# Side work of a finished chunk handed out as a pipeline of stages

## The chip, the core and the metric

The kernel runs on one NeuronCore of a Trainium2 chip. The metric is device time in microseconds (us) of the whole program. Engines: TensorE (PE, matrix products; PEld are its weight loads), VectorE (DVE), ScalarE (ACT), GpSimdE (POOL), and SyncE (SP), which here issues every DMA.

## The reference

One encoder layer and a final normalisation, for two groups of tokens (512 and 1024 of them, width 1024) with shared weights. What matters here, for the hidden state `h` of one group:

```python
h = h + jnp.concatenate([o_attn, o_pool], axis=-1) @ w_out
m = _rmsnorm(h, norm_mlp_g)
h = h + jnp.square(jax.nn.relu(m @ w_up)) @ w_down
gate = jax.nn.sigmoid((_rmsnorm(h, norm_ple_g) @ w_ple_gate).astype(jnp.float32)).astype(h.dtype)
h = h + gate * (p_i @ w_ple_proj)
return _rmsnorm(h, final_norm_g)
```

All inputs are float32. `w_up` is 1024 x 4096, `w_down` 4096 x 1024.

## The kernel before

**Chunks and pairs.** The 1536 tokens stand as three chunks of 512: chunk 0 is the first group, chunks 1 and 2 the second. After attention and the output projection comes the MLP, the longest stage: for each chunk 16 *pairs* (two 128-row blocks of `w_up` each), 48 in all, in `for n, pair in enumerate(pairs)`. Below, pair (1,3) is pair 3 of chunk 1. A pair makes seven products of 2 x 2 blocks (tiles `px`, `py`, `pz`, `pq` in PSUM, 12 matmuls each), in the order 1, 6, 2, 5, 7, 3, 4; every float32 operand is split into a rounded high part and the rest, so that one product of blocks is three matmuls. `px`, `pz` and `pq` take two products each, and an engine has to read the first result out before the second is started: ACT with `u` (L941) for `px`, DVE with `u` (L956) for `pz` and with `c` (L961) for `pq`. In chunks 1 and 2 the down projection works on two pairs at a time (class `Double`); its products `pd` (24 matmuls) follow every second product of a pair, 3 of them in an even pair and 4 in an odd one.

**Side work.** Everything else is side work beside these products. It is written as Python generators; those in the queue `chores` are advanced one `yield` at a time by `step()`, which `after(i)` calls once behind each product of chunks 1 and 2. So the position of a `yield` says behind which product an instruction stands. Four generators matter. `finishing(0)` starts in pair (1,1): for each of four 128 x 1024 tiles of chunk 0 it multiplies by the squared norm factor `ws` (DVE, L1352), adds the saved `h` (POOL, L1354), stores the tile (SP, L1356), squares it and makes the high part of the gate's input (ACT, L1358 and L1332), makes its low part (DVE, L1334) and sums the squares (POOL, L1363). `make_m(2)` follows it and prepares chunk 2's inputs; it ends with four reciprocals (DVE, L632). `finishing_from(1)` starts in pair (2,2) and does for chunk 1's four block tiles `H` what `finishing(0)` does, with `lower_from` (POOL adds, L660 and L665; DVE scaling, L651) and `square_from`. `raise_late(2)` adds chunk 2's saved `h`. `stat_h(2, ve)` runs in the gate stage. The two finishing generators end with `spread_g`, which calls `rsqrt_rows`: four small matmuls `ssg`, a scaling (DVE, L537), the root and a split (POOL, L538 to L549), two diagonal tiles `dgg` (DVE, L552), two matmuls `bcg`, a copy `bcs` (ACT, L714).

**What sets the order.** PE, DVE, ACT and POOL run their instructions in the order in which the program writes them (`manual_schedule`). The order on SP's queue is made by a planner: a load is placed not before the matmul it was written behind, a store when the planner expects its data. On the chip each queue is worked off in order, so an instruction that waits holds all that stands behind it. Tiles live in 49 equal slots of on-chip memory; a load also waits for a free slot. In chunks 1 and 2 the split up-weights are loaded ready-made (`w<-kept_d`, one load for each product).

Of the kernel before, what the change touches and what calls it, by code (L numbers as in the profile page):

```python
# [9 lines left out]
F32 = mybir.dt.float32  # L10
# [8 lines left out]
P = 128  # L19
D = 1024  # L20
# [15 lines left out]
def encoder_layer(ctx, tc, xT, xn, xr, pT, w1, w2, w_pool, w_out, w_up, w_down, w_gate, w_proj,  # L36
# [478 lines left out]
    def wait(n):  # L515
        for _ in range(n):
            yield
# [10 lines left out]
    def rsqrt_rows(parts, w, name):  # L528
# [8 lines left out]
        ve.tensor_scalar(r[:, :n], ss[:, :n], 1.0 / D, EPS, op0=ALU.mult, op1=ALU.add)  # L537
        gp.tensor_tensor(r[:, :n], r[:, :n], mhalf[:, :n], op=ALU.pow)  # L538
# [11 lines left out]
        dg = slot([P, 2, w], F32R, f"dg{name}")  # L550
        for i in range(2):
            ve.tensor_tensor(dg[:, i].rearrange("p (a b) -> p a b", a=n), id_sb.unsqueeze(1).to_broadcast(spread),  # L552
                             as32(rh[:, i, :n]).unsqueeze(2).to_broadcast(spread), op=ALU.mult)
# [21 lines left out]
    def make_m(c, et, el):  # L575
# [53 lines left out]
        for b in range(4):  # L629
            yield  # L630
            w = acc[:, 1, b * P:(b + 1) * P]
            ve.reciprocal(w, w)  # L632
        sy.dma_start(w_d[c], acc[:, 1])
# [19 lines left out]
    def lower_from(c, nm, e):  # L653
        H = HS[c]
        r = rest(c, nm) if c < 2 else None
        for a in range(2):
            part = slice(a * CH, (a + 1) * CH)
            t = H[nm][:, part]
            if nm != "11":
                e.tensor_tensor(t, t, H["u"][:, part], op=ALU.add)  # L660
                yield
            scaled(c, nm, a)
            yield
            if r is not None:
                e.tensor_tensor(t, t, r[:, part], op=ALU.add)  # L665
                yield

# [5 lines left out]

    def raise_late(c):
        w = slot([P, CH], F32, f"wr{c}")
        load(w, wr_d)
        for nm in ("22", "11", "12", "21"):
            r = rest(c, nm)
            yield from wait(4)
            for a in range(2):  # L680
                part = slice(a * CH, (a + 1) * CH)
                t = quarters(r[:, part])
                ve.tensor_tensor(t, t, w[:, TOK[nm[1]]].unsqueeze(1).to_broadcast([P, 2, HF]), op=ALU.mult)
                yield
                gp.tensor_tensor(HS[c][nm][:, part], HS[c][nm][:, part], r[:, part], op=ALU.add)
                yield

    def square_from(c, nm, acc):
        sq = slot([P, 4, HF], F32, f"sqh{c}{nm}")
        to = acc[:, 0, TOK[nm[1]]]  # L690
        sc.activation(sq, quarters(HS[c][nm]), AF.Square)
        yield
        gp.tensor_tensor(sq[:, 0:2], sq[:, 0:2], sq[:, 2:4], op=ALU.add)
        yield
        if nm[0] == "1":
            gp.tensor_tensor(to, sq[:, 0], sq[:, 1], op=ALU.add)
# [646 lines left out]
    def finishing(c):  # L1343


        acc = slot([P, 2, CH], F32, f"sqg{c}")
        for a in range(4):
            h = hT[c][a]
            r = slot([P, 2, CH], F32, f"rest{c}{a}")
            load(r, h_d[c][a])  # L1350
            for e in range(2):
                ve.tensor_tensor(h[:, e], h[:, e], ws[c], op=ALU.mult)  # L1352
                yield
                gp.tensor_tensor(h[:, e], h[:, e], r[:, e], op=ALU.add)  # L1354
                yield
            sy.dma_start(hl_d[c][a], h)  # L1356
            sq = slot([P, 2, CH], F32, f"sqg{c}{a}") if a else acc
            sc.activation(sq, h, AF.Square)  # L1358
# [12 lines left out]
        gp.tensor_tensor(acc[:, 0], acc[:, 0], acc[:, 1], op=ALU.add)
        yield from wait(6)
        yield from spread_g(c, acc)

    def finishing_from(c):

        acc = slot([P, 2, CH], F32, f"sqg{c}")
        for nm in ("11", "21", "12", "22"):
            yield from lower_from(c, nm, gp)
            for a in range(2):  # L1380
                t = quarters(HS[c][nm][:, a * CH:(a + 1) * CH])
                sy.dma_start(hl_d[c][2 * (int(nm[0]) - 1) + a][:, :, TOK[nm[1]]], t)
            yield from square_from(c, nm, acc)
# [290 lines left out]
```

## Time and profile before

| | |
|---|---|
| median of 3 timed runs | 1790.66 us (1788.73, 1790.66, 1796.28) |
| the profiled execution, its own time | 1798.7 us |
| its span, first to last instruction | 1796.9 us |
| PE busy | 1735.9 us, 97% of the span |
| DVE, POOL, ACT busy | 1261.6, 1063.9, 908.7 us |
| mean granted PE clock | 0.990 |
| DMA | 389.68 MB, mean 217 GB/s |
| chunk 0's, 1's and 2's pairs start at | 580.9, 915.2, 1245.7 us of the span |
| gate stage starts at | 1585.1 us |

An engine's busy time is the time in which one of its instructions was running; a wait shows as idle time in front of an instruction, with what ended it (its releaser) behind an arrow. In the rows of a timeline, `x12` counts equal instructions merged into one row. In the rows of windows the columns are the stretch, its length, then busy time and (x instructions) of PE, PEld, DVE, ACT and POOL, the granted PE clock, the DMA share and GB/s.

### The profile page before, as it was taken

How to read it: one execution, taken by the hardware profiler on the slowest of the kernel's cores; microseconds unless marked ns; L12 is line 12 of the kernel's file. 1: busy time of each engine (PE TensorE's matmuls, PEld its weight loads, DVE VectorE, ACT ScalarE, POOL GpSimd, SP SyncE). 2: the span in 40 equal slices, each digit the busy share in tenths (PEclk: the TensorE clock that was granted, in tenths of full speed). 3: DMA queues.
4: the chain of work that ended last, by engine and by line, in shares of the span. 5: the costliest groups of instructions: out<-in, count | busy, mean ns of one | idle time of the engine just before them, and what ended most of it. 6: DMA issues, size and time to landing. Idle time of an engine off the chain costs nothing. (4 is left out here: it accounts for less than half of the span.)

```text
span 1796.9 us, 31417 instructions
## 1 busy us (share of the span) xinstructions
PE 1735.9 (97%) x11692; PEld 1579.1 (88%) x11692; DVE 1261.6 (70%) x1788; ACT 908.7 (51%) x1730; POOL 1063.9 (59%) x931
## 2 busy tenths in 40 slices
PE   9999999999999999999999999999999999999997
PEld 6888777888878898889899999999999999987797
DVE  5776865888896577775547766778766666675755
ACT  6344455768794655654535445554444444443232
POOL 3484873545674767765636756796676565652421
PEclk9999999999999999999999999999999999999998
DMA  6232645120428789897899776989667787732102
GB/s 250 95 129 101 227 164 181 54 95 13 160 75 325 275 294 371 318 326 263 279 392 337 276 267 218 329 282 386 236 240 258 271 265 264 262 139 102 59 13 83
DMA packets 133032, 389.68 MB, mean 217 GB/s; under 512 B 14096, under 2 KB 26768, under 8 KB 132880
## 3 DMA queue, kind: packets, MB, share of 16 engines
q1 hardware_dynamic: 132880, 387.68, 60.2%
q8 instruction: 92, 1.51, 0.3%
q14 instruction: 60, 0.49, 0.1%
HBM read 273.86 MB, written 113.77 MB: 216 GB/s over the span
## 5 line engine op out<-in xcount | busy, mean ns | idle before, releaser
L49 PE MATMUL pd<-ta,v 128*128 128x256 f32 x2688 | 340.6, 283 | 2.4 <-POOL v L1009 1.9
L49 PEld LDWEIGHTS pd<-ta,v 128*128 128x128 f32 x2688 | 330.6, 191 | 3.5 <-POOL v L1009 2.3
L1009 POOL TENSOR_TENSOR v<-we,v 128x512 fp32r<-128x512 f32 x128 | 185.0, 1467 | 103.4 <-DVE ta L1029 26.0
L1009 POOL TENSOR_TENSOR v<-vs,v 128x512 fp32r<-128x512 f32 x96 | 128.7, 1363 | 111.5 <-DVE c L1032 37.2
L49 PE MATMUL pd<-r,wd 128*128 128x512 f32 x768 | 190.6, 396 | 2.4 <-DVE r L926 2.3
L461 POOL TENSOR_SCALAR pr<-pr,rr 128x512 f32<-128x512 f32 x160 | 111.7, 709 | 133.9 <-DVE rr L456 67.2
L49 PE MATMUL z<-w,x 128*128 128x512 f32 (+1 forms) x864 | 175.0, 358 | 2.2 <-ACT x L124 0.9
L1029 DVE TENSOR_TENSOR ta<-c,ta 128x512 fp32r<-128x512 f32 x112 | 108.1, 965 | 88.4 <-ACT ta L1027 82.1
L49 PEld LDWEIGHTS pd<-r,wd 128*128 128x128 f32 x768 | 140.3, 189 | 31.8 <-DVE r L926 3.3
L49 PEld LDWEIGHTS z<-w,x 128*128 128x128 f32 x864 | 142.4, 188 | 29.2 <-ACT w L159 2.5
L49 PE MATMUL px<-mo,w 128*128 128x256 f32 x1152 | 154.4, 284 | 9.4 <-ACT u L941 9.4
L49 PE MATMUL pz<-mo,w 128*128 128x256 f32 x1152 | 154.8, 284 | 5.1 <-DVE u L956 4.9
L49 PE MATMUL pq<-mo,w 128*128 128x256 f32 x1152 | 153.9, 283 | 4.6 <-DVE c L961 2.9
L49 PEld LDWEIGHTS px<-mo,w 128*128 128x128 f32 x1152 | 145.4, 190 | 12.9 <-ACT u L941 11.3
L49 PEld LDWEIGHTS pz<-mo,w 128*128 128x128 f32 x1152 | 147.3, 191 | 9.1 <-DVE u L956 5.8
L49 PEld LDWEIGHTS pq<-mo,w 128*128 128x128 f32 x1152 | 144.4, 190 | 5.7 <-DVE c L961 3.7
L820 POOL TENSOR_TENSOR w<-ws,w 128x512 fp32r<-128x512 f32 x72 | 101.8, 1418 | 73.9 <-ACT w L819 61.9
L49 PE MATMUL pg<-hg,wg 128*128 128x512 f32 (+1 forms) x768 | 144.2, 344 | 0.0
L49 PEld LDWEIGHTS pg<-hg,wg 128*128 128x128 f32 x768 | 121.6, 193 | 17.4 <-DVE s L1519 0.3
L472 ACT CAST pt<-tp 128x512 fp32r<-128x512 f32 x160 | 88.0, 591 | 88.6 <-PE tp L53 86.8
L473 DVE TENSOR_TENSOR pt<-tp,pt 128x512 fp32r<-128x512 f32 x160 | 104.0, 684 | 31.3 <-ACT pt L472 31.0
L441 DVE TENSOR_REDUCE nm<-S 128x1 f32<-128x1024 f32 (+1 forms) x96 | 100.0, 1042 | 23.3 <-PE S L49 22.7
(262 smaller groups left out, 3529.4 us busy)
## 6 DMA issues: line engine op xcount, KB each, us to landing
w<-kept_d SPq DMA_DIRECT2D x210, 512.0 KB, 5.7
kept_d<-w SPq DMA_DIRECT2D x105, 512.0 KB, 4.8
we<-in_w_down_dram SPq DMA_DIRECT2D x64, 512.0 KB, 5.9
mo_d<-mm SPq DMA_DIRECT2D x84, 256.0 KB, 4.1
mo<-mo_d SPq DMA_DIRECT2D x42, 512.0 KB, 9.9
wur<-in_w_up_dram SPq DMA_DIRECT2D x36, 512.0 KB, 5.7
wdr<-in_w_down_dram SPq DMA_DIRECT2D x32, 512.0 KB, 6.8
h_d<-h SPq DMA_DIRECT2D x16, 512.0 KB, 2.9
```

The lines of the kernel that those rows point to most:

```text
L49: last_pe[0] = nc.tensor.matmul(*a, **k).ins
L441: ve.tensor_reduce(nm, S[:, :nch * CH], axis=AX.X, op=ALU.max, negate=True)
L461: gp.tensor_scalar(p, p, rr, 1.0, op0=ALU.mult, op1=ALU.mult)
L472: sc.copy(self.pt[kt][:, 0], tp)
L473: ve.tensor_tensor(self.pt[kt][:, 1], tp, as32(self.pt[kt][:, 0]), op=ALU.subtract)
L820: gp.tensor_tensor(t[:, 1], x, as32(t[:, 0]), op=ALU.subtract)
L1009: ins = gp.tensor_tensor(lo[:, p], src[:, p], as32(hi[:, p]), op=ALU.subtract).ins
L1029: last_ve[0] = ve.tensor_tensor(t[:, 1], x, as32(t[:, 0]), op=ALU.subtract).ins
```

## The change

The four generators are rewritten. `staged(items, *stages)` takes tiles and stages; in round t it runs the last stage on an early tile, then the stage before on the next tile, and so on, so that one tile's multiplication, addition, squaring and summing stand in different rounds, with other tiles' steps between them. The saved `h` of a tile is loaded a round or more before the addition that reads it. `lower_from` and `square_from` are replaced by stages. In `make_m` the reciprocals write to the half `acc[:, 0]` of their tile, which the earlier sums used, and no longer in place of `acc[:, 1]`, which chunk 2 also stores to `wr_d`. In `rsqrt_rows`, for chunks 0 and 1 (`g0`, `g1`), one `yield` stands between scaling and root and two between root and diagonal. The number of steps changes: `finishing(0)` has 42 in place of 44 to its end, `finishing_from(1)` 48 in place of 44, `raise_late(2)` 20 in place of 32.

```diff
--- before.py
+++ after.py
@@ -535,6 +535,8 @@
                           start=i == 0, stop=i == len(parts) - 1)
         r = small.tile([P, 4], F32, tag="rs", name=f"rs{name}", bufs=2)
         ve.tensor_scalar(r[:, :n], ss[:, :n], 1.0 / D, EPS, op0=ALU.mult, op1=ALU.add)
+        if name in ("g0", "g1"):
+            yield
         gp.tensor_tensor(r[:, :n], r[:, :n], mhalf[:, :n], op=ALU.pow)
         spread = [P, n, P]
         if len(parts) > 1:
@@ -548,6 +550,8 @@
         gp.tensor_scalar(rh[:, 0, :n], r[:, :n], 1.0, 1.0, op0=ALU.mult, op1=ALU.mult)
         gp.tensor_tensor(rh[:, 1, :n], r[:, :n], as32(rh[:, 0, :n]), op=ALU.subtract)
         dg = slot([P, 2, w], F32R, f"dg{name}")
+        if name in ("g0", "g1"):
+            yield from wait(2)
         for i in range(2):
             ve.tensor_tensor(dg[:, i].rearrange("p (a b) -> p a b", a=n), id_sb.unsqueeze(1).to_broadcast(spread),
                              as32(rh[:, i, :n]).unsqueeze(2).to_broadcast(spread), op=ALU.mult)
@@ -628,9 +632,9 @@
             sy.dma_start(wr_d, acc[:, 1])
         for b in range(4):
             yield
-            w = acc[:, 1, b * P:(b + 1) * P]
-            ve.reciprocal(w, w)
-        sy.dma_start(w_d[c], acc[:, 1])
+            part = slice(b * P, (b + 1) * P)
+            ve.reciprocal(acc[:, 0, part], acc[:, 1, part])
+        sy.dma_start(w_d[c], acc[:, 0])
 
     def load_mo(c, i):
         MO[c, i] = [slot([P, 4, HF], F32R, f"mo{c}_{i}{j}") for j in range(2)]
@@ -649,21 +653,6 @@
     def scaled(c, nm, a):
         t = quarters(HS[c][nm][:, a * CH:(a + 1) * CH])
         ve.tensor_tensor(t, t, ws[c][:, TOK[nm[1]]].unsqueeze(1).to_broadcast([P, 2, HF]), op=ALU.mult)
-
-    def lower_from(c, nm, e):
-        H = HS[c]
-        r = rest(c, nm) if c < 2 else None
-        for a in range(2):
-            part = slice(a * CH, (a + 1) * CH)
-            t = H[nm][:, part]
-            if nm != "11":
-                e.tensor_tensor(t, t, H["u"][:, part], op=ALU.add)
-                yield
-            scaled(c, nm, a)
-            yield
-            if r is not None:
-                e.tensor_tensor(t, t, r[:, part], op=ALU.add)
-                yield
 
     def rest(c, nm):
         r = slot([P, D], F32, f"rest{c}{nm}")
@@ -671,39 +660,71 @@
             load(quarters(r[:, a * CH:(a + 1) * CH]), h_d[c][2 * (int(nm[0]) - 1) + a][:, :, TOK[nm[1]]])
         return r
 
+    def staged(items, *stages):
+        for t in range(len(items) + len(stages) - 1):
+            for s in reversed(range(len(stages))):
+                if 0 <= t - s < len(items):
+                    yield from stages[s](items[t - s])
+
+    HALVES = (slice(0, CH), slice(CH, D))
+
     def raise_late(c):
         w = slot([P, CH], F32, f"wr{c}")
         load(w, wr_d)
-        for nm in ("22", "11", "12", "21"):
-            r = rest(c, nm)
-            yield from wait(4)
-            for a in range(2):
-                part = slice(a * CH, (a + 1) * CH)
-                t = quarters(r[:, part])
+        r = {}
+
+        def fetch(nm):
+            r[nm] = rest(c, nm)
+            yield
+
+        def scale(nm):
+            for part in HALVES:
+                t = quarters(r[nm][:, part])
                 ve.tensor_tensor(t, t, w[:, TOK[nm[1]]].unsqueeze(1).to_broadcast([P, 2, HF]), op=ALU.mult)
                 yield
-                gp.tensor_tensor(HS[c][nm][:, part], HS[c][nm][:, part], r[:, part], op=ALU.add)
+
+        def add(nm):
+            for part in HALVES:
+                gp.tensor_tensor(HS[c][nm][:, part], HS[c][nm][:, part], r[nm][:, part], op=ALU.add)
                 yield
 
-    def square_from(c, nm, acc):
-        sq = slot([P, 4, HF], F32, f"sqh{c}{nm}")
-        to = acc[:, 0, TOK[nm[1]]]
-        sc.activation(sq, quarters(HS[c][nm]), AF.Square)
-        yield
-        gp.tensor_tensor(sq[:, 0:2], sq[:, 0:2], sq[:, 2:4], op=ALU.add)
-        yield
-        if nm[0] == "1":
-            gp.tensor_tensor(to, sq[:, 0], sq[:, 1], op=ALU.add)
-        else:
-            gp.tensor_tensor(to, to, sq[:, 0], op=ALU.add)
-            gp.tensor_tensor(to, to, sq[:, 1], op=ALU.add)
-        yield
+        yield from staged(("22", "11", "12", "21"), fetch, scale, add)
+
+    def squares(c, acc):
+
+        sqs = {}
+
+        def square(nm):
+            sqs[nm] = slot([P, 4, HF], F32, f"sqh{c}{nm}")
+            sc.activation(sqs[nm], quarters(HS[c][nm]), AF.Square)
+            yield
+
+        def total(nm):
+            sq, to = sqs[nm], acc[:, 0, TOK[nm[1]]]
+            gp.tensor_tensor(sq[:, 0:2], sq[:, 0:2], sq[:, 2:4], op=ALU.add)
+            yield
+            if nm[0] == "1":
+                gp.tensor_tensor(to, sq[:, 0], sq[:, 1], op=ALU.add)
+            else:
+                gp.tensor_tensor(to, to, sq[:, 0], op=ALU.add)
+                gp.tensor_tensor(to, to, sq[:, 1], op=ALU.add)
+            yield
+
+        return square, total
 
     def stat_h(c, e):
         acc = slot([P, 2, CH], F32, f"sqg{c}")
-        for nm in ("11", "21", "12", "22"):
-            yield from lower_from(c, nm, e)
-            yield from square_from(c, nm, acc)
+
+        def lower(nm):
+            for a, part in enumerate(HALVES):
+                t = HS[c][nm][:, part]
+                if nm != "11":
+                    e.tensor_tensor(t, t, HS[c]["u"][:, part], op=ALU.add)
+                    yield
+                scaled(c, nm, a)
+                yield
+
+        yield from staged(("11", "21", "12", "22"), lower, *squares(c, acc))
         yield from wait(8)
         yield from spread_g(c, acc)
 
@@ -1342,32 +1363,42 @@
     hl_d = [[dram.tile([P, 2, CH], F32, name=f"hl_d{c}_{a}") for a in range(4)] for c in range(2)]
     def finishing(c):
 
-
         acc = slot([P, 2, CH], F32, f"sqg{c}")
-        for a in range(4):
-            h = hT[c][a]
-            r = slot([P, 2, CH], F32, f"rest{c}{a}")
-            load(r, h_d[c][a])
+        r, sqs = {}, {}
+
+        def fetch(a):
+            r[a] = slot([P, 2, CH], F32, f"rest{c}{a}")
+            load(r[a], h_d[c][a])
+            if not a:
+                yield
+
+        def scale(a):
             for e in range(2):
-                ve.tensor_tensor(h[:, e], h[:, e], ws[c], op=ALU.mult)
+                ve.tensor_tensor(hT[c][a][:, e], hT[c][a][:, e], ws[c], op=ALU.mult)
                 yield
-                gp.tensor_tensor(h[:, e], h[:, e], r[:, e], op=ALU.add)
+
+        def add(a):
+            for e in range(2):
+                gp.tensor_tensor(hT[c][a][:, e], hT[c][a][:, e], r[a][:, e], op=ALU.add)
                 yield
-            sy.dma_start(hl_d[c][a], h)
-            sq = slot([P, 2, CH], F32, f"sqg{c}{a}") if a else acc
-            sc.activation(sq, h, AF.Square)
-            if c == 0:
-                gate_in(0, a, True)
-            yield
-            for e in range(2) if a else ():
-                gp.tensor_tensor(acc[:, e], acc[:, e], sq[:, e], op=ALU.add)
+            sy.dma_start(hl_d[c][a], hT[c][a])
+
+        def square(a):
+            sqs[a] = slot([P, 2, CH], F32, f"sqg{c}{a}") if a else acc
+            sc.activation(sqs[a], hT[c][a], AF.Square)
+            gate_in(0, a, True)
+            yield
+
+        def total(a):
+            for e in range(2):
+                if a:
+                    gp.tensor_tensor(acc[:, e], acc[:, e], sqs[a][:, e], op=ALU.add)
+                gate_in(0, a, False, (e,))
                 yield
-            if c == 0:
-                for e in range(2):
-                    gate_in(0, a, False, (e,))
-                    yield
-                for i in range(2):
-                    sy.dma_start(hg_d[a][i], flat(gin[c, a][i]))
+            for i in range(2):
+                sy.dma_start(hg_d[a][i], flat(gin[c, a][i]))
+
+        yield from staged(range(4), fetch, scale, add, square, total)
         gp.tensor_tensor(acc[:, 0], acc[:, 0], acc[:, 1], op=ALU.add)
         yield from wait(6)
         yield from spread_g(c, acc)
@@ -1375,12 +1406,29 @@
     def finishing_from(c):
 
         acc = slot([P, 2, CH], F32, f"sqg{c}")
-        for nm in ("11", "21", "12", "22"):
-            yield from lower_from(c, nm, gp)
+        H, r, sqs = HS[c], {}, {}
+
+        def fetch(nm):
+            r[nm] = rest(c, nm)
+            if nm == "11":
+                yield
+            for part in HALVES:
+                if nm != "11":
+                    gp.tensor_tensor(H[nm][:, part], H[nm][:, part], H["u"][:, part], op=ALU.add)
+                    yield
+
+        def scale(nm):
             for a in range(2):
-                t = quarters(HS[c][nm][:, a * CH:(a + 1) * CH])
-                sy.dma_start(hl_d[c][2 * (int(nm[0]) - 1) + a][:, :, TOK[nm[1]]], t)
-            yield from square_from(c, nm, acc)
+                scaled(c, nm, a)
+                yield
+
+        def add(nm):
+            for a, part in enumerate(HALVES):
+                gp.tensor_tensor(H[nm][:, part], H[nm][:, part], r[nm][:, part], op=ALU.add)
+                yield
+                sy.dma_start(hl_d[c][2 * (int(nm[0]) - 1) + a][:, :, TOK[nm[1]]], quarters(H[nm][:, part]))
+
+        yield from staged(("11", "21", "12", "22"), fetch, scale, add, *squares(c, acc))
         yield from wait(6)
         yield from spread_g(c, acc)
 
```

Line numbers move by up to 50: L941, L956, L961, L1358, L1356 of before are L962, L977, L982, L1388, L1384 of the change; L1009, L1029 and L1060 (POOL `v`, DVE `ta`, DVE `H`) are L1030, L1050 and L1081. Three places, as the built programs have them.

**ACT, pairs (1,2) and (1,3):** the squaring of chunk 0's second tile `h01m` (`sqg<-h01m`); `ta`, `v` and `H` belong to the down products. Before:

```order
L1027 CAST ta_0_3_10682<-c_01_10229 128x512
L1003 CAST v_0_30_10684<-vs_00_10505 128x1024
L1057 COPY H_10731<-pd_05_10692 128x1024
L1358 ACTIVATE sqg_10737<-h01m 128x1024
L1332 ACTIVATE hg_0_10739<-h01m,gple_sb 128x512 x2
L966 ACTIVATE c_10_10570<-c_10_10570 128x256
L967 ACTIVATE c_10_10570<-c_10_10570 128x256
L1027 CAST ta_0_7_10762<-c_00_10228 128x512
L1003 CAST v_0_70_10764<-we_001_10376 128x1024
```

Now:

```order
L993 ACTIVATE c_11_10568<-c_11_10568 128x512
L994 ACTIVATE c_11_10568<-c_11_10568 128x512
L962 COPY u_3_10812<-px_3_10813 128x256
L1048 CAST ta_0_6_10831<-c_00_10228 128x512
L1024 CAST v_0_60_10833<-vs_01_10554 128x1024
L1388 ACTIVATE sqg_10866<-h01m 128x1024
L1353 ACTIVATE hg_0_10868<-h01m,gple_sb 128x512 x2
L1078 COPY H_10885<-pd_05_10691 128x1024
L971 ACTIVATE c_10_10567<-px_3_10813 128x256
L972 ACTIVATE c_10_10567<-c_10_10567 128x256
```

It moved behind the next pair's `u_3<-px_3`, ten instructions later; the POOL addition that it needs moved forward.

**POOL and SP, pairs (1,1) and (1,2):** the additions to `h00m`, and on SP the store `hl_d_0<-h00m` among the loads `w_2_*` of pair (1,2)'s seven products. POOL before:

```order
L820 TENSOR_TENSOR w_0_4_10294<-wur_01_9976,w_0_4_10294 128x512
L1354 TENSOR_TENSOR h00m<-h00m,rest_10431 128x512 x2
L1009 TENSOR_TENSOR v_0_11_10507<-we_000_10327,v_0_10_10506 128x512 x2
L1009 TENSOR_TENSOR v_0_51_10559<-vs_00_10505,v_0_50_10558 128x512 x2
L1009 TENSOR_TENSOR v_0_21_10613<-we_010_10467,v_0_20_10612 128x512 x2
```

Now:

```order
L841 TENSOR_TENSOR w_0_4_10294<-wur_01_9976,w_0_4_10294 128x512
L1382 TENSOR_TENSOR h00m<-h00m,rest_10431 128x512
L1030 TENSOR_TENSOR v_0_11_10508<-we_000_10327,v_0_10_10507 128x512 x2
L1382 TENSOR_TENSOR h00m<-h00m,rest_10431 128x512
L1030 TENSOR_TENSOR v_0_51_10556<-vs_00_10506,v_0_50_10555 128x512 x2
```

SP before:

```order
L56 DMA w_2_1_10484<-kept_d_1_324 128x1024
L56 DMA w_2_6_10501<-kept_d_6_325 128x1024
L1356 DMA hl_d_0_6645<-h00m 128x1024
L56 DMA w_2_2_10534<-kept_d_2_326 128x1024
L56 DMA w_2_5_10552<-kept_d_5_327 128x1024
L1370 DMA hg_d_6653<-hg_0_10515 128x1024
L56 DMA w_2_7_10566<-kept_d_7_328 128x1024
L56 DMA w_2_3_10568<-kept_d_3_329 128x1024
L56 DMA w_2_4_10587<-kept_d_4_330 128x1024
```

Now:

```order
L56 DMA w_2_1_10483<-kept_d_1_324 128x1024
L56 DMA rest_10485<-h_d_1_306 128x1024
L56 DMA w_2_6_10502<-kept_d_6_325 128x1024
L56 DMA w_2_2_10530<-kept_d_2_326 128x1024
L1384 DMA hl_d_0_6645<-h00m 128x1024
L56 DMA w_2_5_10549<-kept_d_5_327 128x1024
L56 DMA w_2_7_10563<-kept_d_7_328 128x1024
L56 DMA w_2_3_10565<-kept_d_3_329 128x1024
L56 DMA w_2_4_10584<-kept_d_4_330 128x1024
```

The second addition moved behind the two `v_0_11`. On SP the store moved one load back, behind `w_2_2`; a load `rest` of the next tile moved ahead of `w_2_6`, and the store `hg_d` moved out of these rows.

**DVE, pair (1,6):** `rsg` (L537) and the diagonal tiles `dgg`. Before:

```order
L965 TENSOR_TENSOR c_30_11604<-pz_6_11691,u_6_11606 128x256
L1029 TENSOR_TENSOR ta_2_7_11780<-c_20_11092,ta_2_7_11780 128x512
L1032 TENSOR_TENSOR c_20_11092<-c_21_11093,c_20_11092 128x2x256
L537 TENSOR_SCALAR rsg_11818<-ssg_11813 128x4
L552 TENSOR_TENSOR dgg_11824<-id_sb,rhg_11821 128x512 x2
L1060 TENSOR_TENSOR H_10808<-pd_21_11649,H_10808 128x1024
L971 TENSOR_TENSOR c_31_11605<-pq_6_11744,u_6_11606 128x256
```

Now:

```order
L537 TENSOR_SCALAR rsg_11629<-ssg_11624 128x4
L967 TENSOR_TENSOR u_6_11606<-py_6_11631,u_6_11606 128x256
L1050 TENSOR_TENSOR ta_2_2_11647<-c_21_11089,ta_2_2_11647 128x512
L1035 TENSOR_TENSOR vs_20_11501<-we_210_11431,vs_21_11572 128x1024
L1081 TENSOR_TENSOR H1u<-pd_21_11656,H1u 128x1024
L977 TENSOR_TENSOR u_6_11606<-pz_6_11703,u_6_11606 128x256
L1027 TENSOR_TENSOR we_201_11278<-we_200_11202,we_201_11278 128x1024
L1050 TENSOR_TENSOR ta_2_3_11721<-c_21_11089,ta_2_3_11721 128x512
L1053 TENSOR_TENSOR c_20_11088<-c_21_11089,c_20_11088 128x2x256
L556 TENSOR_TENSOR dgg_11685<-id_sb,rhg_11682 128x512 x2
L1081 TENSOR_TENSOR H_10731<-pd_25_11731,H_10731 128x1024
```

Between scaling and diagonal stand eight other instructions now; before there was none.

## The prediction

> **What bounds the kernel now.** I read the page's busy times first, then PE's waits, then windows of one pair each, then timelines around PE's gaps. PE is busy for 97% of the span; the other 61 us, and what follows from them, are all that a new order of the side work can win. In PE's waits (total us, times, longest us) these three belong to the MLP of chunks 1 and 2:
>
> ```profile
> PE px L49 <- ACT u L941: 9.4, 8, 2.9
> PE pz L49 <- DVE u L956: 4.9, 3, 2.2
> PE pq L49 <- DVE c L961: 2.9, 4, 2.0
> ```
>
> Each is PE waiting until a first product has been read out of PSUM. Pair by pair (each window runs from one pair's first `px` matmul to the next pair's), in order (1,2), (1,3), (1,4), (1,5), (1,7), (1,8), (1,15), (2,4), (2,5), (2,6), (2,11):
>
> ```profile
> 946.15:964.68 18.53, 18.53 (x158) 18.53 (x157) 17.05 (x17) 9.46 (x15) 13.82 (x9) 1.00 0.92 338
> 964.68:990.79 26.11, 23.17 (x183) 22.97 (x181) 17.71 (x21) 15.31 (x25) 17.70 (x13) 0.93 0.85 322
> 990.79:1009.94 19.15, 18.80 (x158) 18.60 (x157) 16.02 (x16) 8.51 (x14) 15.44 (x10) 1.00 0.68 234
> 1009.94:1035.45 25.51, 23.36 (x182) 23.04 (x181) 16.27 (x19) 11.21 (x19) 16.57 (x12) 0.93 0.86 320
> 1054.89:1080.55 25.66, 23.61 (x185) 23.18 (x183) 14.40 (x20) 10.30 (x18) 11.98 (x11) 0.93 0.65 224
> 1080.55:1099.09 18.54, 18.54 (x158) 18.54 (x157) 11.86 (x16) 11.52 (x20) 12.56 (x10) 1.00 0.63 204
> 1221.61:1245.70 24.09, 21.90 (x183) 21.49 (x181) 19.29 (x22) 9.67 (x16) 14.54 (x10) 1.00 0.97 375
> 1327.85:1349.56 21.71, 19.05 (x159) 18.65 (x157) 16.24 (x18) 10.71 (x18) 17.47 (x13) 1.00 0.52 179
> 1349.56:1371.37 21.81, 21.68 (x183) 21.48 (x181) 13.71 (x17) 9.08 (x15) 14.63 (x11) 1.00 0.91 325
> 1371.37:1394.98 23.61, 20.59 (x159) 20.18 (x157) 17.06 (x19) 10.63 (x18) 17.00 (x13) 0.93 0.65 224
> 1476.13:1497.49 21.36, 21.36 (x182) 21.36 (x181) 14.68 (x20) 9.75 (x17) 12.40 (x10) 1.00 0.79 273
> ```
>
> An even pair without a stall takes 18.54 us, an odd one 21.36. Pair (1,3) is 4.75 over that, (1,4) 0.61, (1,5) 4.15, (1,15) 2.73, (2,4) 3.17, (2,5) 0.45, (2,6) 5.07. The timeline of (1,3) shows why:
>
> ```profile
> 966.59 1.06 ACT L1358 ACTIVATE sqg<-h01m 128x1024 f32<-128x1024 f32 x1 [7.80 <-POOL h01m L1354]
> 968.97 1.60 PE L49 MATMUL py<-mo,w 128*128 128x256 f32 x12
> 973.50 2.00 PE L49 MATMUL px<-mo,w 128*128 128x256 f32 x12 [2.94 <-ACT u L941]
> 975.30 4.26 PE L49 MATMUL pd<-ta,v 128*128 128x256 f32 x24
> 982.27 3.00 PE L49 MATMUL pd<-ta,v 128*128 128x256 f32 x24
> ```
>
> ACT stood 7.80 us at the square of `h01m`, whose POOL addition had not come; the copy `u` was queued behind it. Between two products of one tile lie another product and one `pd` block (1.60 and 3.00 us, overlapping a little, so about 4.3), which is how late a reader may be for nothing. And the stall costs more than its idle time: the `pd` block behind it took 4.26 us, the later one 3.00, because the granted clock (column behind POOL's) had halved:
>
> ```profile
> 975.50:977.50 2.00, 2.00 (x12) 2.00 (x11) 2.00 (x2) 1.97 (x5) 2.00 (x2) 0.50 1.04 417
> ```
>
> The four pairs with a clock of 0.93 are those with a gap of 2.05 us or more. Excess less idle is 4.75 - 2.94 = 1.8 and, with the next fence's 2.15, 4.15 - 2.15 = 2.0: 1.9 for a halved clock.
>
> **The change part by part.** The other stalls, in order of time:
>
> ```profile
> 1028.14 2.02 PE L49 MATMUL pz<-mo,w 128*128 128x256 f32 x12 [2.15 <-DVE u L956]
> 1058.66 1.48 DVE L552 TENSOR_TENSOR dgg<-id_sb,rhg 128x512 fp32r<-128x512 f32 x2 [3.94 <-POOL rhg L548]
> 1063.24 2.81 PE L49 MATMUL px<-mo,w 128*128 128x256 f32 x12 [2.05 <-ACT u L941]
> 1225.05 0.95 DVE L632 RECIPROCAL sqm<-sqm 128x128 f32<-128x128 f32 x1 [2.21 <-DMA wr_d<-sqm]
> 1229.05 1.68 PE L49 MATMUL px<-mo,w 128*128 128x256 f32 x12 [1.60 <-ACT u L941]
> 1348.03 1.69 PE L49 MATMUL pq<-mo,w 128*128 128x256 f32 x12 [1.99 <-DVE c L961]
> 1373.97 0.69 DVE L651 TENSOR_TENSOR H<-H,w 128x512 f32<-128x512 f32 x1 [2.94 <-POOL H L660]
> 1387.65 2.93 PE L49 MATMUL pz<-mo,w 128*128 128x256 f32 x12 [2.14 <-DVE u L956]
> ```
>
> *Stages in `finishing(0)`.* Addition and square now stand two to five steps apart. A step is 18.54 / 7 = 2.6 us, so the 7.80 us wait has nothing left. I take the whole excess of (1,3), (1,4), (1,5): 4.75 + 0.61 + 4.15 = 9.5.
>
> *Root and diagonal.* DVE's 3.94 us at `dgg` (pair (1,7)) become two steps, 5.3 us, filled with other work. Gone: 2.05 + 1.9 = 3.95. For `g1` there was no PE stall: nothing.
>
> *Reciprocal.* Its target is no longer what `wr_d` reads, so DVE's 2.21 us go. I take PE's idle alone, 1.6; the rest of (1,15) stays, since it is at the next chunk's weights.
>
> *Stages in `finishing_from(1)`.* DVE no longer scales right behind POOL's addition: 3.17 + 0.45 + 5.07 = 8.7.
>
> Together 9.5 + 3.95 + 1.6 + 8.7 = 23.7. No instruction is added or removed.
>
> *What becomes late: a load.* In SP's new order the store `hl_d_0` stands ahead of `w_2_5`, `w_2_7`, `w_2_3`, `w_2_4`, and it waits for POOL's second addition, now queued behind two `v_0_11`. The rows, of the timeline and of the page's DMA issues (last column: us to landing):
>
> ```profile
> 940.63 1.29 POOL L1354 TENSOR_TENSOR h00m<-h00m,rest 128x512 f32<-128x512 f32 x1 [0.63 <-DVE h00m L1352]
> 941.95 0.32 SPq L1356 DMA_DIRECT2D hl_d<-h00m  x1
> 942.36 1.23 SPq L56 DMA_DIRECT2D w<-kept_d  x2
> 945.81 2.99 POOL L1009 TENSOR_TENSOR v<-we,v 128x512 fp32r<-128x512 f32 x2 [3.89 <-DVE ta L1029]
> 953.27 1.59 PE L49 MATMUL pz<-mo,w 128*128 128x256 f32 x12
> ...
> w<-kept_d SPq DMA_DIRECT2D x210, 512.0 KB, 5.7
> mo<-mo_d SPq DMA_DIRECT2D x42, 512.0 KB, 9.9
> ```
>
> The addition would end at 945.81 + 2.99 + 1.29 = 950.1 in place of 941.9; the load behind the store goes out 0.4 later, at 950.5, and lands at 956.2. Product 5 of pair (1,2) began at 953.27: PE waits 2.9 us, and with the halved clock loses 4.8. Ends: 0, if the load lands in 2.8 us less than the median, and 9, if it takes 9.9 us. I take 4.8, as POOL's order is fixed and the store needs both halves. Pair (1,2) has no stall before.
>
> *Other moved transfers.* Each `rest` of `finishing(0)` and `finishing_from(1)` now goes out a round earlier on SP, ahead of one or two `w` loads, and each `hl_d` store a place or two later; none is added. Two loads are issued in 1.23 us (the row above), so a `w` load behind one more `rest` leaves 0.6 us later. A PE wait would need several of these at once; I put it under the 2 us below.
>
> *Loads used sooner.* `raise_late` no longer waits four steps behind its loads, which stand seven places later on SP, behind `w_9_3`. Before, that load went out at:
>
> ```profile
> 1432.19 3.19 SPq L56 DMA_DIRECT2D w<-kept_d  x2
> 1439.67 0.68 DVE L1032 TENSOR_TENSOR c<-c,c 128x512 f32<-128x512 f32 x1
> ```
>
> Now `wr` and `rest` go right behind it, by some 1433.5, and land by 1439.2; DVE's multiplication comes behind the `c` row, at 1440.4. Cost nothing; if the loads are 4.3 us later still, the readers' slack covers them, beyond that each us is one of PE.
>
> *Moved work that may collide.* `make_m(2)` comes two steps earlier, and DVE's side work stands closer. Pair (1,2) ran without a stall at 17.05 of 18.53 us DVE busy, so 92% is borne. I charge 2 us, about one small stall like the 1.60; ends 0 and 6 (three with 2 us each). In the gate stage the sum ends in the same step: 0.
>
> Sum: 23.7 - 4.8 - 2 = 16.9. The profiled execution (1798.7 us, 8 above the median) would come to 1781.8, the median from 1790.66 to **1774**.
>
> **Rivals.** (a) *The clock does not halve in the timed runs.* They are shorter than the profiled execution, and gaps of 2.05 to 2.15 stand close to the 1.99 that kept its clock. Then 4 x 1.9 = 7.6 less is won and the load's stall costs 2.9: 23.7 - 7.6 - 2.9 - 2 = 11.2, 1779.5. The Trainium skill speaks for it (TensorE: Matmul & The Clock Gate, section "Why this matters for your kernels": the clock falls to half after idle gaps above about 3 us); the trace disagrees, with 0.50 behind 2.94 us and 0.93 for a pair behind 2.05.
>
> (b) *The readers are late from load, not from waiting.* DVE is busy 16 to 18 us in the bad pairs, against 11.86 in (1,8). If half the excess returns elsewhere: 11.9 - 4.8 = 7.1, 1783.6. Against it: the rows name a wait ahead of each stall.
>
> (c) *The stores hold up the loads each time*, so that the change only moves the stall: four `hl_d_0` to `hl_d_3` at 4.8 each, 23.7 - 19.2 - 2 = 2.5, 1788. Against it: SP stood 8.5 us at such a store before, without a late load:
>
> ```profile
> SPq L1356 <- POOL h02m L1354: 8.5, 1, 8.5
> ```
>
> (d) *Slower.* The same in chunk 1 for the eight stores of the gate's input too: each tile's earlier `rest` takes a slot, so loads go out with less lead, and each store then stops them. Eight of twelve stores at 4.8 cost 38.4: 1790.66 - 23.7 + 2 + 38.4 = 1807. It decides from seven on (33.6 > 23.7 + 9).
>
> **How the numbers follow.** Forecast 0.56, (a) 0.12, (b) 0.13, (c) 0.13, (d) 0.06. This kernel can tell about 0.5%, 9 us. Faster than 1781.7: 0.55 of the forecast, 0.10 of (a), 0.06 of (b), 0.71. Slower than 1799.6: (d) and a remainder, 0.07. Same: 0.22. Range: 1764 (no load stall, none of the 2 us, and 3 us more) to 1788, which takes in (a), (b), the dear end of the load and the middle of (c).
>
> **What would show it.** Right: no `sqg` row of ACT behind POOL for over 2 us, no `dgg` behind `rhg`, no reciprocal behind `wr_d`; pairs (1,3), (1,5), (1,7), (2,4), (2,6) within 1 us of 18.54 or 21.36 plus the small matmuls; one PE wait for `w<-kept_d` in pair (1,2). Wrong: these pairs still at a clock of 0.93, or several waits for loads.

## The result, and the profile after

The change took 1781.48 us (median of 8, 1777.01 to 1789.48) where the kernel before took 1791.38 in the same comparison: a ratio of 0.9937, 95% interval 0.9915 to 0.996, or 11.3 us (7.2 to 15.2). Timed again with five rounds it was 1783.26 against 1794.98, 0.9935 (0.9923 to 0.9948). So it is faster by some 0.6%, two thirds of the 16.9 us that were forecast, and 1781.5 lies in the range of 1764 to 1788. The profiled execution took 1782.3 us, its span is 1780.6.

PE's waits of the change, for the MLP (total us, times, longest):

```profile
PE px L49 <- ACT u L962: 5.4, 3, 3.9
PE pq L49 <- DVE c L982: 2.5, 3, 1.2
PE pz L49 <- DMA w<-kept_d: 2.2, 1, 2.2
ACT ta L1048 <- DMA mo_d<-mm: 9.0, 3, 5.0
```

Late readers cost PE 17.2 us before and 7.9 now. New are one wait for a load and, on ACT, the wait of a `ta` for a store. Windows of single pairs of the change, in order (1,2), (1,4), (1,5), (1,7), (1,13), (1,15), (2,0), (2,5), (2,6):

```profile
945.77:968.24 22.47, 20.28 (x158) 20.11 (x157) 19.13 (x19) 13.80 (x22) 17.78 (x11) 0.92 0.78 292
989.61:1009.68 20.07, 18.85 (x159) 18.65 (x158) 17.35 (x18) 9.91 (x15) 16.15 (x11) 1.00 0.87 307
1009.68:1032.02 22.34, 21.64 (x183) 21.43 (x181) 19.94 (x22) 13.47 (x23) 18.88 (x13) 1.00 1.00 377
1051.88:1073.24 21.36, 21.36 (x182) 21.35 (x180) 12.36 (x18) 10.77 (x19) 9.72 (x8) 1.00 0.74 250
1172.53:1200.62 28.09, 24.23 (x183) 24.02 (x182) 14.46 (x18) 13.32 (x24) 21.03 (x16) 0.88 0.92 316
1219.85:1241.19 21.34, 21.34 (x182) 21.34 (x181) 18.71 (x22) 10.05 (x18) 16.71 (x12) 1.00 0.95 366
1241.19:1259.77 18.58, 18.58 (x159) 18.58 (x158) 16.13 (x15) 9.38 (x17) 14.98 (x10) 1.00 0.90 338
1339.69:1362.24 22.55, 21.67 (x182) 21.46 (x181) 16.84 (x20) 9.89 (x16) 16.29 (x14) 1.00 0.83 292
1362.24:1381.99 19.75, 18.88 (x159) 18.67 (x157) 17.22 (x15) 9.62 (x16) 18.87 (x13) 1.00 0.56 184
```

Pair (1,7) is clean, and so are (1,3) and (2,4), which took 21.37 and 18.57 us. Pair (1,2) has the forecast load stall; (1,4), (1,5), (2,5) and (2,6) stay 1.0 to 1.5 us over 18.54 or 21.36, which in (1,4) and (2,5) is more than before (0.6 and 0.45 us); (1,13) takes 28.1 us where it took 22.3; (2,0), 20.84 before, is clean, which was not forecast. By place, from the two first profiles (a kernel with one part alone is in the last column; negative is shorter):

| place | forecast | change | alone |
|---|---|---|---|
| stages of `finishing(0)`, pairs (1,3) to (1,5) | -9.5 | -7.0 | -7.0 |
| steps between root and diagonal, (1,7) | -3.95 | -4.3 | -3.8, and +3.4 in (1,6) |
| reciprocal, (1,15) | -1.6 | -2.75 | -2.3 |
| stages of `finishing_from(1)`, (2,4) to (2,6) | -8.7 | -6.3 | -6.4 |
| load behind `hl_d_0`, (1,2) | +4.8 | +3.9 | +2.4 |
| collisions: (1,6) +0.4, (1,10) to (1,14) +5.6, (2,0) -2.3 | +2 | +3.7 | |

The column of the change sums to -12.7. From pair (1,0) to the gate stage the change is 10.8 us shorter (670.0 and 659.2 us). Of the 2 us between the two, 1.4 are pair (2,15), 29.4 us before and 30.8 in the change: its clock halved from 1570.41 to 1573.82, behind gaps of 0.46 and 1.05 us that the kernel before has too. The second profiles of both kernels have it the other way round (30.8 and 29.4), so this is chance. The gate stage is 5.2 us shorter as well (211.8 and 206.6 us), and that is not the change, as the next section shows.

### The profile page after: what moved, and what is told of

Same layout as the page of the kernel before. It is cut to its first block, busy times and chain, and to the rows that moved or that the text cites. A ratio compares the mean times of both kernels' runs of the same rounds, so it can differ in the third digit from the quotient of the medians.

```text
span 1780.6 us, 31418 instructions
## 1 busy us (share of the span) xinstructions
PE 1730.1 (97%) x11692; PEld 1576.6 (89%) x11692; DVE 1266.7 (71%) x1788; ACT 909.8 (51%) x1730; POOL 1068.6 (60%) x931
## 5 line engine op out<-in xcount | busy, mean ns | idle before, releaser
L1030 POOL TENSOR_TENSOR v<-we,v 128x512 fp32r<-128x512 f32 x128 | 186.8, 1480 | 94.5 <-DVE ta L1050 30.9
L1030 POOL TENSOR_TENSOR v<-vs,v 128x512 fp32r<-128x512 f32 x96 | 130.1, 1376 | 106.7 <-DVE c L1053 38.5
L1050 DVE TENSOR_TENSOR ta<-c,ta 128x512 fp32r<-128x512 f32 x112 | 110.2, 984 | 87.1 <-ACT ta L1048 79.7
L49 PE MATMUL pg<-hg,wg 128*128 128x512 f32 (+1 forms) x768 | 140.3, 337 | 0.0
```

The lines of the kernel that those rows point to most:

```text
L49: last_pe[0] = nc.tensor.matmul(*a, **k).ins
L1030: ins = gp.tensor_tensor(lo[:, p], src[:, p], as32(hi[:, p]), op=ALU.subtract).ins
L1050: last_ve[0] = ve.tensor_tensor(t[:, 1], x, as32(t[:, 0]), op=ALU.subtract).ins
```

## The experiments

**The kernel before, a second time**

> The kernel before, unchanged, profiled a second time. Its first profiled execution (1798.7 us) was the slow end of its times, the median is 1791.4. Theory: PE's gaps come back as they were (2.94, 2.15, 2.05, 1.60, 1.99, 2.14 us in the MLP, 1.91 and 1.69 in the gate stage), but the clock halves behind only some of those of 1.7 to 2.2 us; each spared one takes 1.6 to 3.5 us off, and the time is 1789 to 1794. Rival: the same gaps halve the clock each time, and the 7 us lie elsewhere (in the stages ahead of the MLP, or in longer gaps).

It took 1790.2 us. The theory held. The gaps came back: 2.95, 2.15, 2.10, 1.10, 1.99 and 2.13 us in the MLP, 1.93 in the gate stage. But behind the 2.10 of pair (1,7) and the 1.93 the clock stayed. In the gate stage of the first profile, then of the second:

```profile
1705.27 1.02 PE L49 MATMUL ssg<-ones_sb,sqg 128*128 128x1 f32 x4 [1.91 <-POOL sqg L699]
1706.15 8.45 PE L49 MATMUL pg<-hg,wg 128*128 128x512 f32 x24
```

```profile
1701.36 0.61 PE L49 MATMUL ssg<-ones_sb,sqg 128*128 128x1 f32 x4 [1.93 <-POOL sqg L699]
1701.83 5.78 PE L49 MATMUL pg<-hg,wg 128*128 128x512 f32 x24
```

The same 24 matmuls took 8.45 us behind a gap of 1.91 and 5.78 behind one of 1.93. That is why the gate stage "lost" 5.2 us: in the second profile, without the change, it takes 207.2. From pair (1,0) to the gate stage the two profiles of the kernel before are alike, 670.0 and 669.4 us, since the 1.5 us spared in (1,7) were lost in (2,15). Another 3.3 us of their difference lie ahead of chunk 1's pairs, and their cause stays open. The halved stretches of one execution all start on a grid of 3.413 us, and what decides is the idle time within one stretch of that grid. Pair (1,7) of the first profile, then of the second, cut on their grids:

```profile
1059.99:1063.41 3.42, 1.37 (x10) 0.94 (x9) 1.62 (x3) 1.74 (x4) 0.00 (x0) 1.00 0.22 70
1063.41:1066.82 3.41, 3.41 (x17) 3.41 (x18) 2.76 (x4) 2.43 (x5) 1.61 (x2) 0.50 1.01 375
```

```profile
1055.57:1058.98 3.41, 2.38 (x19) 1.94 (x17) 2.74 (x4) 0.54 (x1) 0.65 (x1) 1.00 0.33 133
1058.98:1062.39 3.41, 2.35 (x19) 2.35 (x20) 1.85 (x3) 3.35 (x8) 0.38 (x1) 1.00 0.81 275
```

In the first, PE's 2.05 idle us lie in one stretch and the next has clock 0.50, with 17 matmuls in 3.41 us. In the second, the gap of 2.10 lies across a border, 1.03 and 1.06 us to each side, and the clock stays. The gap of 1.99 that kept its clock in the first profile was cut in the same way, 0.66 us ahead of the border and 1.32 behind it:

```profile
1343.30:1346.71 3.41, 2.75 (x24) 2.54 (x22) 2.23 (x3) 0.00 (x0) 3.41 (x3) 1.00 0.88 289
1346.71:1350.13 3.42, 2.10 (x17) 2.10 (x18) 1.98 (x4) 1.75 (x4) 2.17 (x2) 1.00 0.10 39
```

Over all 14 profiles of this study, from the MLP on, stretches at full clock with 1.9 us or more of idle PE were followed by a halved one 46 times of 46, those with 1.75 to 1.9 us 8 of 9, with 1.4 to 1.75 us 14 of 40, with 1.0 to 1.4 us 1 of 28. So a gap of about 2 us halves the clock or not by where it falls. The Trainium skill (TensorE: Matmul & The Clock Gate, section "What's actually happening") tells of a free-running window of 3413 ns, and the trace agrees with that figure; that an idle time of more than about 3 us is needed, as its section "Why this matters for your kernels" has it, these runs contradict: half a window is enough.

**Where `make_m(2)` stands.** Two kernels: the change with `make_m(2)` put back, and the kernel before with nothing but `make_m(2)` moved. The first, at the end of `finishing(0)`:

```diff
         yield from spread_g(c, acc)
+        yield from wait(2)
```

> The change, with two empty steps at the end of finishing(0), so that make_m(2) stands where it stood before; nothing else moves ahead of it. Theory: the 3.86 us gap of pair (1,13) comes from make_m(2) standing two steps earlier; the pair goes from 28.1 back to the 22.3 of before, the gaps of (1,10) and (1,12) come back as before (0.2, 0.5), and the chunk boundary, which had gained 2.3 us in (2,0), loses it again; sum about -4 us. Rival: the stall comes from the tiles that finishing(0) in stages keeps, and stays at 26 us or more.

The second, in `make_m`:

```diff
-            yield from wait(5)
+            yield from wait(3 if (c, b) == (2, 0) else 5)
```

> The kernel before, with nothing but make_m(2) two steps earlier (its first wait is 3 steps in place of 5). Theory: that alone makes pair (1,13) stall by 3 to 4 us of idle time (28 us in place of 22.3), and that alone brings the 2.3 us of the chunk boundary and pair (2,0). Rival: alone it does neither, since it takes the tiles of the staged finishing(0) as well.

Pairs (1,13) and (2,0) of the kernel before (its second profile); (1,13), (1,15) and (2,0) of the change with `make_m(2)` back; then (1,13), (1,15) and (2,0) of the kernel before with `make_m(2)` early:

```profile
1175.41:1197.72 22.31, 21.73 (x183) 21.52 (x181) 14.32 (x19) 13.95 (x25) 18.50 (x14) 1.00 0.89 293
1240.29:1261.15 20.86, 19.46 (x158) 18.78 (x157) 18.45 (x19) 10.21 (x19) 17.18 (x11) 1.00 0.82 312
```

```profile
1172.73:1194.99 22.26, 21.71 (x182) 21.50 (x181) 14.37 (x19) 14.03 (x25) 18.45 (x14) 1.00 0.85 294
1214.01:1235.83 21.82, 21.66 (x182) 21.46 (x181) 19.23 (x22) 9.78 (x16) 14.56 (x10) 1.00 1.02 394
1235.83:1256.67 20.84, 19.39 (x159) 18.72 (x158) 18.41 (x19) 10.22 (x19) 17.17 (x11) 1.00 0.85 325
```

```profile
1179.48:1205.66 26.18, 23.22 (x183) 23.02 (x181) 14.07 (x17) 12.22 (x22) 19.93 (x16) 0.93 0.91 311
1224.94:1246.30 21.36, 21.36 (x183) 21.36 (x181) 18.73 (x21) 9.02 (x15) 16.20 (x11) 1.00 0.95 362
1246.30:1265.88 19.58, 19.12 (x158) 18.67 (x157) 17.15 (x18) 10.31 (x19) 16.00 (x11) 1.00 0.88 341
```

The two kernels agree: the place of `make_m(2)` makes the stall of (1,13), without stages in `finishing(0)`, and it makes the gain in (2,0), 1.3 of the 2.3 us in the kernel before. It also clears (1,15), 23.6 to 24.1 us before, to 21.36 without any change to the reciprocals; so in the change either edit would have removed that stall, the reciprocals all but 0.4 us of it. In (1,13) it costs 3.9 (26.18 against 22.31 of the second profile before) to 5.8 us, over pairs (1,10) to (2,0) together 1.9 in the kernel before (147.28 against 145.35) and 2.0 in the change (146.58 against 144.54). The first took 1778.6 us, the second 1794.2, one time each. How the stall comes about, read from the timeline of the change:

```profile
1168.16 5.64 SPq L620 DMA_DIRECT2D mo_d<-mm  x3
1172.17 1.29 POOL L618 TENSOR_TENSOR mm<-m,mm 128x512 fp32r<-128x512 f32 x1
1176.67 0.62 ACT L1048 CAST ta<-c 128x512 fp32r<-128x512 f32 x1 [3.04 <-DMA mo_d<-mm]
1181.82 0.36 ACT L962 COPY u<-px 128x256 f32<-128x256 f32 x1
1182.24 2.93 PE L49 MATMUL px<-mo,w 128*128 128x256 f32 x12 [3.86 <-ACT u L962]
```

`ta`, the operand of the next down product, takes a slot that held an `mm` tile, and that is free only when the `mm` tile's store has landed. The store stood on SP until POOL's subtraction was through (1173.5), landed at 1176.6, and `ta`, then DVE's part of it, `c`, and in the end ACT's `u` came later. The wait `ACT ta <- DMA mo_d<-mm` is in no profile with `make_m(2)` at its old place. A wait of this kind does not make a stall by itself: in the change a `ta` of (1,10) waits 5.0 us for such a store, and PE's gap there is 0.44; in the kernel before a `u` of (1,14) waits 3.1 us, and PE has no gap. That the slot is the cause is read from the rows; no kernel gave that `ta` another slot.

**Both additions in one step**

```diff
                 gp.tensor_tensor(hT[c][a][:, e], hT[c][a][:, e], r[a][:, e], op=ALU.add)
-                yield
+                if a:
+                    yield
             sy.dma_start(hl_d[c][a], hT[c][a])
+            if not a:
+                yield from wait(2)
```

> The change, with both additions of the first tile h00m in one step and its store behind them; two empty steps behind it, so that all else keeps its step. Theory: the second addition no longer stands behind two v, the store leaves SP at about 943 instead of 950.2, and pair (1,2) goes from 22.5 to 18.5 us. Rival: another load is late then, or the reader of that pair, and the pair stays over 20.5 us.

It took 1778.3 us. Pair (1,2) of it:

```profile
944.29:963.72 19.43, 18.77 (x158) 18.57 (x157) 17.04 (x17) 11.93 (x19) 16.14 (x10) 1.00 0.94 353
```

The store left SP at 941.5 in place of 950.2. So the forecast stall was the store's: 3.0 of its 3.9 us are gone, and the clock is whole. 0.66 us stay as a gap, so the theory's 18.5 was not quite reached, and pair (1,4) takes 0.4 us more (20.46, its gap 1.62 us in place of 1.22).

**One part at a time.** `finishing(0)` alone, with `yield from wait(5)` behind `spread_g`:

> The kernel before with finishing(0) alone in stages, and five empty steps at its end so that make_m(2) keeps its place. Theory: pairs (1,3) to (1,5), 70.8 us before, come to 63.8 as in the change, not to the 61.3 that the prediction took, since the left-over gaps of (1,4) and (1,5) (1.2 and 0.7 us) are made by this part itself; pair (1,2) takes the load's 3.9 us; (1,7), (1,13), (1,15) and chunk 2 stay as before. Sum -3 us. Rival: the left-over gaps come from the other parts, and the three pairs take 62 us or less.

The steps at root and diagonal alone, with `wait(3)` in place of `wait(6)` ahead of `spread_g`:

> The kernel before with the steps between scaling, root and diagonal alone, three empty steps less ahead of them, so that make_m(2) keeps its place. Theory: pair (1,7) goes from 25.7 (24.2 in the second profile) to 21.4 us, and nothing else moves by over 0.5. Rival: the late reader of (1,7) comes from the closer side work, and some 1 us of gap stays.

The reciprocal's three lines of the change alone:

> The kernel before with the reciprocal beside the stored tile alone. Theory: it removes the gap of 1.1 to 1.6 us in pair (1,15) and leaves 0.2 to 0.6 there, but not the gaps of (2,0) (0.4 and 0.9), which went with make_m(2) two steps earlier; pair (1,15) 21.8, (2,0) 20.8. Rival: both go, pair (2,0) comes to 18.6, and the earlier make_m(2) was no part of it.

`finishing_from`, `raise_late` and `stat_h` of the change alone:

> The kernel before with finishing_from(1), raise_late(2) and stat_h alone in stages. Theory: pairs (2,4) to (2,6), 67.1 us before, come to 60.9 as in the change, chunk 1 stays as before, raise_late's earlier use of its loads costs nothing, and the gate stage keeps its gaps of 0.78, 0.85, 1.9 and 1.7 us. Rival: the prediction's 58.4 us for the three pairs, what is left in the change (0.9 us of gap in (2,5) and in (2,6)) coming from the other parts.

They took 1784.9, 1794.9, 1795.8 and 1788.5 us; one time each tells little, the pairs tell more. Of the first, pairs (1,2) and (1,4); of the second, (1,6) and (1,7); of the third, (1,15) and (2,0); of the fourth, (2,5) and (2,6):

```profile
946.30:967.29 20.99, 18.77 (x159) 18.60 (x157) 18.78 (x17) 12.48 (x21) 18.37 (x11) 1.00 0.76 281
988.66:1008.74 20.08, 18.84 (x158) 18.64 (x157) 17.36 (x19) 9.91 (x15) 16.16 (x11) 1.00 0.88 315
```

```profile
1036.46:1059.30 22.84, 21.22 (x167) 21.02 (x165) 16.89 (x22) 9.87 (x17) 13.14 (x12) 0.93 0.78 276
1059.30:1081.12 21.82, 21.82 (x184) 21.73 (x183) 14.26 (x19) 10.31 (x18) 10.15 (x8) 1.00 0.76 248
```

```profile
1222.74:1244.54 21.80, 21.64 (x183) 21.44 (x181) 19.20 (x22) 9.77 (x16) 14.56 (x10) 1.00 1.03 402
1244.54:1265.39 20.85, 19.43 (x158) 18.73 (x157) 18.43 (x19) 10.21 (x19) 17.16 (x11) 1.00 0.83 319
```

```profile
1347.19:1369.70 22.51, 21.67 (x182) 21.46 (x181) 16.79 (x20) 9.87 (x16) 16.24 (x14) 1.00 0.84 300
1369.70:1389.43 19.73, 18.79 (x159) 18.59 (x157) 17.20 (x15) 9.62 (x16) 18.86 (x13) 1.00 0.56 188
```

The stages leave their own rest: (1,4) at 20.08, (2,5) and (2,6) at 22.51 and 19.73, as in the change. The load's stall of (1,2) comes with `finishing(0)` alone; its gap is 2.22 us, and with the clock at 1.00 the pair loses 2.4 in place of 3.9. The reciprocal clears its gap in (1,15) and does nothing for (2,0). The second kernel is half a miss: no reader is late at the diagonal in (1,7), but (1,6), 19.44 before, stalled by 1.62 us with a halved clock. Its row among PE's waits names the cause:

```profile
PE ssg L49 <- POOL sqg L1375: 1.6, 1, 1.6
```

With three empty steps taken out ahead of `spread_g`, its first matmul `ssg` came to stand before POOL had finished the last sum `sqg`. The change keeps `wait(6)` there and has no such wait in the MLP; the stall belongs to this experiment. Pair (1,15) lost 1.1 us too (25.17, a gap of 2.05), which had not been expected either. What the new steps cost or win by themselves is thus known for (1,7) only.

**Mended versions.** The change was timed again beside them:

> The change, unchanged, timed and profiled again beside the two below. Theory: 1777 to 1783 us, 0.992 to 0.996 of before; gaps of pairs (1,2), (1,4), (1,13), (2,5), (2,6) as in the first profile to 0.7 us, with a halved clock behind some of those over 1.7 us. Rival: one of these stalls (the 3.86 us of pair (1,13) first of all, whose cause is a store's time to landing) is of that one execution only.

Both mends together, `make_m(2)` back and the first tile's additions in one step:

> The change with both additions of h00m in one step and make_m(2) put back by two steps. Theory: pair (1,2) 19.4, (1,13) 22.3, while (1,12), (1,15) and (2,0) take 0.9, 0.4 and 2.3 us more than in the change; in all 4 to 6 us less than the change, 1774 to 1777. Rival: the two mends meet (another order on SP makes another load late) and the time is within 2 us of the change.

The same with the end of `make_m(2)` two steps earlier:

```diff
-        yield from wait(7)
+        yield from wait(5 if c == 2 else 7)
         bc = tp_ps(f"w{c}")
```

> The kernel of both_mended, with only the end of make_m(2) two steps earlier (the statistics matmul, the four reciprocals and the store of the norm factor; its wait is 5 steps in place of 7). Theory: the 2.3 us of pair (2,0) and the 0.4 of (1,15) come from that end alone, so they go again and (1,13) stays at 22.3: 2 to 3 us less than both_mended. Rival: they come from the earlier stores of chunk 2's inputs, mo_d, and (2,0) stays at 20.8.

And both mends with one empty step in place of two:

> The kernel of both_mended with one empty step at finishing(0)'s end in place of two, so that make_m(2) stands one step earlier than before. Theory: (1,13)'s stall needs a ta whose place an mm gives free only by its store; each step of make_m(2) makes another pairing, so the stall is not a matter of more or less: with one step the wait of ta for the stores is either there (pair over 25 us) or not (22 to 23), and the gain of (2,0) comes with the earlier stores in part (19.5 to 20.5 us). Time 1775 if it is not there, 1779 if it is. Rival: the stall grows evenly with the shift, 24 to 25.5 us at one step, and the time is equal to both_mended to 2 us.

| kernel | median us | of before, 95% interval |
|---|---|---|
| change | 1783.26 | 0.9935 (0.9923 to 0.9948) |
| both mends | 1776.50 | 0.9899 (0.9886 to 0.9913) |
| end of `make_m(2)` earlier | 1775.44 | 0.9898 (0.9883 to 0.9913) |
| one step in place of two | 1775.91 | 0.9899 (0.9882 to 0.9917) |

Pair (1,13) with both mends, (2,0) with the earlier end, and (1,13) and (2,0) with one step:

```profile
1170.10:1192.40 22.30, 21.70 (x183) 21.50 (x181) 14.06 (x18) 13.63 (x24) 18.50 (x14) 1.00 0.87 296
```

```profile
1233.48:1254.34 20.86, 19.44 (x159) 18.77 (x157) 18.45 (x19) 10.20 (x19) 17.21 (x11) 1.00 0.90 346
```

```profile
1170.24:1192.44 22.20, 21.60 (x182) 21.40 (x181) 14.49 (x17) 10.58 (x19) 18.51 (x14) 1.00 0.90 328
1233.74:1254.76 21.02, 19.42 (x158) 18.75 (x157) 18.60 (x20) 10.22 (x19) 17.29 (x11) 1.00 0.85 325
```

Both mends win another 6.8 us on the change, by the medians, a little over the 4 to 6 that were expected. The three mended versions can't be told apart. The earlier end did not bring back the gain of (2,0), so that gain does not come from the end of `make_m(2)` alone; which of its earlier instructions brings it stays open. At one step the stall of (1,13) is wholly gone and does not grow evenly with the shift, as if it hung on which tile meets which slot. But a `ta` still waits once for such a store (2.6 us) without PE waiting for it, and (2,0) gained nothing, so of the theory only the all-or-nothing held. In the change's second profile (1,13) has a gap of 3.83 us and (1,2) one of 3.05 (2.19 in the first): they are no accidents of one execution.

## Why the prediction was right, and where it was off

*What bounds, and where.* PE's gaps behind late readers were the right things to count, and the waits named by the rows were their causes. In the profile of the change `sqg` doesn't wait for POOL, `dgg` not for `rhg` (but for 3.3 us in the gate stage, where the change adds no step), no reciprocal for `wr_d`; (1,3), (1,7), (1,15) and (2,4) have no gap. In (1,15) the forecast left the 1.1 us beyond the 1.6 standing; they went too, and as `make_m(2)` early clears that pair alone, the reciprocals' share in it can't be told.

*The load behind `hl_d_0`.* Forecast: PE 2.9 us late, 4.8 us lost. Measured:

```profile
945.44 3.00 POOL L1030 TENSOR_TENSOR v<-we,v 128x512 fp32r<-128x512 f32 x2 [3.73 <-DVE ta L1050]
948.40 1.75 POOL L1382 TENSOR_TENSOR h00m<-h00m,rest 128x512 f32<-128x512 f32 x1
950.17 0.32 SPq L1384 DMA_DIRECT2D hl_d<-h00m  x1
950.58 2.21 SPq L56 DMA_DIRECT2D w<-kept_d  x4
```

The addition ended at 950.15, the load went out at 950.58, PE waited 2.19 us in one profile and 3.05 in the other, and the pair lost 3.9 and 4.8 us.

*The step that failed:* "I take the whole excess of (1,3), (1,4), (1,5)", and the same for 8.7 in chunk 1. Of these 18.2 us, 13.3 went; 4.9 are left or came new, and the kernels with one part alone show that the stages themselves leave them. Rival (b), readers late from load and not from waiting, was right for this quarter. That is most of the 6.1 us by which the 10.8 of the MLP fall short of the forecast. The rows of (1,4) show the load at work:

```profile
1001.43 3.98 POOL L1382 TENSOR_TENSOR h03m<-h03m,rest 128x512 f32<-128x512 f32 x2
1002.48 1.78 DVE L1050 TENSOR_TENSOR ta<-c,ta 128x512 fp32r<-128x512 f32 x1
1004.18 1.78 DVE L1053 TENSOR_TENSOR c<-c,c 128x512 f32<-128x512 f32 x1
1007.69 0.41 DVE L982 TENSOR_TENSOR c<-pq,u 128x256 f32<-128x256 f32 x1
1008.15 1.69 PE L49 MATMUL pq<-mo,w 128*128 128x256 f32 x12 [1.22 <-DVE c L982]
```

No wait for a releaser makes `c` late: from 996.9 to 1008.1 DVE runs one instruction after the other. DVE's two instructions take 1.78 us each while POOL adds; their median over the kernel is 0.69 and 0.68 us. The 2.2 us lost so are more than the gap of 1.22. That the overlap is the cause of this gap is read from the rows and was not tried by itself.

*"I charge 2 us" for collisions.* The size came near by luck; the content was wrong. What moved is `make_m(2)`, two steps early: +5.8 in (1,13), and against that (2,0) and others, 2.0 net in the change. I had looked at DVE's load there; what stalls is a slot held by a store.

*The halved clock, 1.9 us for each of four gaps, and the profile against the median.* The price per halving is about right: (1,2) lost 1.7 to 1.8 us beyond its gap in the two profiles of the change. But whether a gap of about 2 us halves the clock is chance. The profiled execution before had caught more halvings in the gate stage than the second one, 4.6 us worth, and stood 7 to 8 us above the median; the profile after stands 0.9 above its own. The forecast carried the 8 us over as if they were constant. The span fell by 16.3 us, close to the 16.9 of the sum, but 5.2 of that are the gate stage's luck, and the timed difference, 11.3, fits the MLP's 10.8 (669.4 and 658.6 us in the second profiles, a difference of the same size). Rival (a), that the clock doesn't halve in timed runs, is wrong as it was put: the second profiled execution before, at 1790.2 us no slower than the median, has four halved stretches between pair (1,0) and the gate stage, as many as the first.

*The other rivals.* (c) and (d) asked for stalls at several stores: PE has one wait for a kept load, at `hl_d_0`. `raise_late`'s loads cost next to nothing: pair (2,8) went from 18.98 to 19.06 us (19.36 with chunk 1's part alone).

## What to carry to other kernels

Before removing a wait, look at what the engine does in that pair besides waiting. The sum of its work doesn't tell: with some 17 us of DVE work, pair (1,2) before was clean (17.05) and pair (1,4) of the change late (17.35). What stands right ahead of the reader tells more, and whether another engine slows it there. When a list of side steps becomes shorter, whatever follows in the queue moves too; pad it to its old length and time the two edits apart. Steps taken out ahead of a consumer can put it before its producer, as `ssg` before `sqg` here. In a kernel whose tiles share slots, a store that frees a slot is a dependency that no data flow shows.

## What had not been expected of the hardware

The clock's halving goes by fixed stretches of 3.413 us and by about half a stretch of idle PE, so a gap of 2 us costs 2 us or up to 4, by chance, from one execution to the next; the gate stages of two profiles of one kernel differed by 4.6 us for this alone. And DVE's 128x512 instruction that takes 0.68 us alone takes up to 1.8 us beside POOL, in the profile of the change:

```profile
L1053 DVE TENSOR_TENSOR c<-c,c x48: 676/683/1785, 961.6 to 1596.4; 128x512 f32<-128x512 f32 x48
```

(shortest, median and longest in ns). Of these 48, the 40 during which POOL ran nothing took 0.69 us at most; the 8 that met a POOL instruction took 1.22 to 1.79. The Trainium skill (GPSIMD Engine Reference, section "1. Specifications") names contention of the two engines for instructions with two inputs in on-chip memory, and the trace agrees; the factor of 2.6 is this kernel's.
